# Stick-breaking attention moved beside the RWKV prelude, and the queued projections multiplied unsplit in fp32

## Chip, core and metric

The kernel runs on one core of a Trainium2 chip, as one program. Its time is device microseconds (us) of one execution; the median of three executions is given. A core has TensorE (PE, matmuls and transposes), VectorE (DVE), ScalarE (ACT), GpSimd (POOL) and SyncE (SP, which issues most transfers here). Each engine runs its own instructions strictly in the order in which the program lists them.

## What is computed

Two blocks follow one another. Only the first is touched. It works on 272 rows (16 meta tokens and 256 tokens) of width 1024:

```python
xn = rms_norm(h, norm_mix[layer])
proj = xn @ w_in[layer]
q_sb, k_sb, v_sb, rw, gate_sb, gate_rw = jnp.split(proj, in_splits, axis=-1)
y_sb = stick_breaking_attention(...)          # 8 heads of 64
rw = token_shift(rw, mu_rw[layer])
r, kr, vr, w_lo, a_lo, g_lo = jnp.split(rw, rw_splits, axis=-1)
...                                           # decay, a, g, kk: the RWKV inputs
y_rw = rwkv7_recurrence(r_h, decay, k_h, v_h, kk, a_h)
y_rw = group_norm_heads(y_rw, ln_x_w[layer], ln_x_b[layer])   # + bonus, times g
merged = (sigmoid(gate_sb) * (y_sb @ w_sb_out[layer])
          + sigmoid(gate_rw) * (y_rw @ w_rw_out[layer]))
h = h + merged @ w_out[layer]                 # then a feed-forward layer
```

Stick-breaking attention, for a query t and a key s < t, weighs v_s with sigmoid(z_ts) times the product of (1 - sigmoid(z_tj)) over the keys between. The second block (two layers of attention and of a product-key expert layer) has the same work before and after.

## The kernel before

A tile scheduler turns the program's text into one fixed list of instructions for each engine; it decides by program order and by a few raised priorities, when the program is built.

**Split projections.** `proj_ws_steps` (L264 to L266) multiplies a weight matrix with the activations. Each step loads 512 KB of weights into a tile `raw` (three buffers). ACT copies it to `hi` in the shorter format fp32r (L221), and DVE (or POOL, with `sub=G`) subtracts to get `lo` (L222). The activations are held as the pair XH, XL in the same way. Every product is three matmuls: XH with hi, XL with hi, XH with lo. With 256 columns such a matmul reads `128x256`, for the 272 rows `128x272`.

**Stage 1, projections and attention.** q, k and v are projected first. Then the four pairs of heads of the stick-breaking attention run: scores (L518 to L525, 256-column products into the PSUM tile `w`), softplus as Abs, Exp, Ln on ACT (L527 to L529) and one DVE instruction, weights (L539), exponent (L549), output (L555 to L560) and a split of it into YH, YL. Between them the queue `K.queue` puts steps of the projections of kr, rr and vr (`FILL = 0, 2, 1` steps at three places of each pair).

**Stage 2, the RWKV prelude.** The last projection, LO (columns 3072 to 3359), gives the low-rank inputs of decay, a and g. Sigmoids (L642), a scan, exponents (L660 to L663), the inverse norm by Ln and Exp (L178, L179) and many elementwise products on DVE give the operands of the recurrence; transposes (L710, L715) and ACT copies end it. Beside it runs the queue with `gate(3360, gs)`, `merge_sb()` and `gate(4384, gr)`: 480 split matmuls in all, called the filler below. Its hi copies are on ACT, its lo subtractions on POOL. The filler's results leave PSUM through a sigmoid on ACT (L593) or a DVE product (L598).

**Stage 3, pairs.** Sixteen groups of products of ART with BZ or KZ (L743), masked by DVE, with the small matmuls of a block inverse between. **Stage 4, inverse chain.** The reduced blocks go to DRAM and back (`d_in`, `MI`), 15 pairs of DVE instructions (L767, L768) invert them row by row, and the result goes to DRAM and back (`d_out`, `XC`); then DVE masks it into TT (L867). **Stage 5, chunk chain.** Unit products (L874), then per 32-row chunk L920, a DVE sum (L921), L930, a DVE sum (L933) and so on, at the end a group norm (L977 to L988) whose result feeds the projection `w_rw_out`. The queue's matmuls stand between the others in stages 2 to 5, wherever the scheduler put them.

Of the kernel before, what the change touches and what calls it, by code (L numbers as in the profile page):

```python
# [8 lines left out]
F = mybir.dt.float32  # L9
FR = mybir.dt.float32r  # L10
# [8 lines left out]
NM = 16  # L19
S = 256  # L20
# [108 lines left out]


FILL = 0, 2, 1
# [5 lines left out]
class Kit:  # L137
# [133 lines left out]

    def proj_nat(self, w, KT, xh, xl, pj, groups, keep=(), done=None, sub=None, gate=(), loaded=None, free=0, idle=0):
# [109 lines left out]
def block1(tc, A, K, dump, finish, outer):  # L382
# [4 lines left out]
    with ExitStack() as es:  # L387
        ps1 = es.enter_context(ExitStack())
        pj = ps1.enter_context(tc.tile_pool(name="pj", bufs=4, space=PSUM))
# [74 lines left out]


        with tc.tile_pool(name="sb", bufs=1) as sb, tc.tile_pool(name="pw", bufs=2, space=PSUM) as pw:
            def wtile():
                return pw.tile([128, 2, 512], F, name="w", tag="w")

            CB = const_part(sb, "end1", "end2", "csb")  # L470
            identb = sb.tile([128, 128], BF, name="identb")
            V.tensor_copy(identb, ident)
            negb = sb.tile([128, 128], BF, name="negb")
            V.tensor_copy(negb, CB("neg"))
            qT = sb.tile([128, 4, S], F, name="qT")
            KZ = sb.tile([128, 2, 4, T], F, name="KZ")
            G.memset(KZ[64:128, 0], 0.0)
            G.memset(KZ[0:64, 1], 0.0)
            KM = sb.tile([128, 4, 128], F, name="KM")
            VM = sb.tile([128, 4, 128], F, name="VM")  # L480
# [12 lines left out]
            K.proj_ws(win, [(1024, 512)], 8, 2, xhT, xlT, T, SUB, lambda j, ps: SC.activation(vTs[:, j], ps, AF.Copy), pj)
            for par in range(2):
                ps = slice(64 * par, 64 * par + 64)
                V.tensor_copy(KM[ps, :, 16 * par:16 * par + 16], KZ[ps, par, :, 0:NM])
                V.tensor_copy(VM[ps, :, 16 * par:16 * par + 16], vTs[ps, :, 0:NM])
            w = wtile()
            for i in range(2):
                for p in range(4):  # L500
                    PE.transpose(w[:, i, p * 128:(p + 1) * 128], vTs[:, p, NM + 128 * i:NM + 128 * (i + 1)], ident)
            V.tensor_copy(VS[:, 0], w[:, 0])
            SC.activation(VS[:, 1], w[:, 1], AF.Copy)
            w = wtile()
            for p in range(4):
                PE.transpose(w[:, 0, p * 128:(p + 1) * 128], VM[:, p], ident)
            V.tensor_copy(VB, w[:, 0].rearrange("p (a b) -> p a b", b=128))
            for c0, dst, mu in ((2048, kr, 20), (1536, rr, 16), (2560, vr, 24)):
                K.queue.append(K.proj_ws_steps(win, [(c0, 512)], 8, 2, xhT, xlT, T, SUB, shift_into(lambda j, dst=dst: dst[:, j], mu), pj))
            ntri, nones = CB("ntri"), CB("nones")  # L510
            parts = lambda x: ([x[:, 256 * r:256 * r + 256] for r in range(2)], [x[:, 512 + 128 * r:640 + 128 * r] for r in range(2)], x[:, 768:1024])

            def sb_scores(p):
                wf = wtile().rearrange("p a b -> p (a b)")
                z0, z1, zm = parts(wf)
                q = qT[:, p]
                for r in range(2):
                    PE.matmul(z0[r], lhsT=KZ[:, r, p, NM:NM + 128], rhs=q, start=r == 0, stop=False)  # L518
                for r in range(2):
                    PE.matmul(z0[r][:, 0:128], lhsT=identb, rhs=negb, start=False, stop=r == 1)  # L520
                for r in range(2):
                    PE.matmul(z1[r], lhsT=KZ[:, r, p, NM + 128:NM + 256], rhs=q[:, 128:256], start=r == 0, stop=False)
                PE.matmul(zm, lhsT=KM[:, p], rhs=q, start=False, stop=False)
                for r in range(2):
                    PE.matmul(z1[r], lhsT=identb, rhs=negb, start=False, stop=r == 1)  # L525
                e = sb.tile([128, 1024], F, name="e", tag="e", bufs=2)
                SC.activation(e, wf, AF.Abs)  # L527
                SC.activation(e, e, AF.Exp, scale=-1.0)
                SC.activation(e, e, AF.Ln, bias=1.0)  # L529
                sp = sb.tile([128, 1024], F, name="sp", tag="sp", bufs=2)  # L530
                V.scalar_tensor_tensor(sp, wf, 0.0, e, op0=OP.max, op1=OP.add)
                return wf, sp

            def sb_weights(wf, sp):
                z0, z1, zm = parts(wf)
                s0, s1, sm = parts(sp)

                def acc(o, l, r, last=False):
                    PE.matmul(o, lhsT=l, rhs=r, start=False, stop=last, skip_group_check=True)  # L539

                for r in range(2):
                    acc(z0[r], ntri, s0[r])
                    acc(z0[r][:, 128:256], nones, s1[r], r == 1)
                    acc(z1[r], ntri, s1[r])
                    acc(zm, CB(f"non{r}"), s0[r])
                    acc(zm[:, 128:256], CB(f"non{r}"), s1[r])
                acc(zm, CB("ntri16"), sm, True)
                a = sb.tile([128, 1024], F, name="a", tag="a")
                SC.activation(a, wf, AF.Exp)  # L549
                return a  # L550

            def sb_out(p, wf, a):
                a0, a1, am = parts(a)
                y = wf[:, 0:S]
                PE.matmul(y, lhsT=VB[:, p], rhs=am, start=True, stop=False)  # L555
                for r in range(2):
                    hs = slice((2 * p + r) * 64, (2 * p + r) * 64 + 64)
                    yr = y[64 * r:64 * r + 64]
                    PE.matmul(yr, lhsT=VS[:, 0, hs], rhs=a0[r], start=False, stop=False)
                    PE.matmul(yr[:, 128:256], lhsT=VS[:, 1, hs], rhs=a1[r], start=False, stop=True)  # L560
                K.split(y, YH[:, p], YL[:, p])
# [12 lines left out]
        dump("ysbh", YH.bitcast(F))  # L574

        gT = b1.tile([128, 4, S], F, name="gT")
        gs = bl.tile([128, 8, S], F, name="gs", tag="gs")
        VN = b1.tile([128, 2, 512], F, name="VN", tag="VN")
        VW = b1.tile([128, 2, 512], F, name="VW")
        LB = b1.tile([128, 2, 2, 512], F, name="LB", tag="LB")  # L580
        RN = b1.tile([128, 2, 2, 8, 64], F, name="RN", tag="RN")
        QT = K.gp.tile([128, 2, 8, 128], F, name="QT", tag="h")
        RT = b1.tile([128, 2, 8, 128], F, name="RT", tag="RT")
        OT = b1.tile([128, 2, 8, 128], F, name="OT", tag="OT")
        pcb = b1.tile([128, 4, 8], F, name="pcb")
        S0 = b1.tile([128, 4, 64], F, name="S0")
        d_in = dr.tile([2, 8, 2048], F, name="d_in")
        d_out = dr.tile([2, 8, 2048], F, name="d_out")

        def gate(c0, dst):  # L590
            for g in range(2):
                K.queue.append(K.proj_ws_steps(win, [(c0 + 512 * g, 512)], 8, 2, xhX, xlX, S, SUB,
                          lambda j, ps, g=g: SC.activation(dst[:, 4 * g + j], ps, AF.Sigmoid), pj, sub=G))  # L593

        def merge_sb():
            for g in range(2):
# [1067 lines left out]
```

## Time and profile before

| what | before |
|---|---|
| time, median of three runs (lowest to highest) | 2433.31 us (2431.47 to 2433.57) |
| the profiled execution's own time | 2431.37 us |
| its span | 2429.6 us |
| mean granted TensorE clock, as a share of 2.4 GHz | 0.988 |
| busy in the span: PE, DVE, ACT, POOL | 2334.9, 1662.0, 1204.5, 241.5 us |

The table is of the whole program. The change touches the first 320 us or so of the span, and there the engines share the time differently than in the rest, so the rows below are read stage by stage. An fp32 matmul stands in the trace as two records, an fp32r matmul as one. The time from the start of one matmul to the start of the next, called its pitch below, is what a matmul costs an engine that is never waiting, because matmuls overlap.

### The profile page before, as it was taken

Reading aid. Unit: us, or ns where it says so; the run is one execution under the profiler, and the core shown is the slowest. Engines: PE = TensorE matmul, PEld = TensorE weight load, DVE = VectorE, ACT = ScalarE, POOL = GpSimd, SP = SyncE. Lnnn points to the kernel's source line nnn. Section 1 sums busy time; section 2 is a strip of 40 time slices with the busy share of each in tenths; the row PEclk is TensorE's granted clock in tenths of the full one; section 3 lists DMA queues with packets and bytes.
Section 4 is the critical chain, followed back from the end, with each engine's and each line's share of the span. In section 5 each row is a group of like instructions: output and inputs, shape, how many; then the busy total and the mean of one; then the engine's idle time right before and its main releaser. Section 6 shows DMA issues by size and latency. Waiting matters only on the chain.

```text
span 2429.6 us, 43499 instructions
## 1 busy us (share of the span) xinstructions
PE 2334.9 (96%) x17012; PEld 2111.7 (87%) x17012; DVE 1662.0 (68%) x3234; ACT 1204.5 (50%) x2118; POOL 241.5 (10%) x253
## 2 busy tenths in 40 slices
PE   8988989998999999999999999899999999999998
PEld 7877869987689999999888877689999999888886
DVE  4478555557779868886555556769968887555555
ACT  4663545444535555545545554534545544455453
POOL 0065400007300000000000003610000000000000
PEclk9998999999999999999999999999999999999999
DMA  5232136564235554545656565315555555555664
GB/s 178 87 110 77 57 122 191 183 202 151 79 113 180 184 175 159 166 156 190 195 194 192 195 201 183 121 62 166 187 181 163 165 159 182 190 191 192 197 192 147
DMA packets 145637, 389.68 MB, mean 160 GB/s; under 512 B 18731, under 2 KB 49510, under 8 KB 145174
## 3 DMA queue, kind: packets, MB, share of 16 engines
q1 hardware_dynamic: 140070, 375.34, 48.3%
q10 hardware_dynamic: 5360, 11.56, 1.5%
q8 instruction: 133, 2.18, 0.4%
q14 instruction: 74, 0.61, 0.1%
HBM read 385.34 MB, written 1.31 MB: 159 GB/s over the span
## 4 chain that ended last, share of the span: by engine, by line
PE 74%; DVE 7%; issue 4%; ACT 2%; DMA 2%; POOL 1%; DVEq 0%; ACTq 0%; POOLq 0%
PE w L1581 27%; PE a L1383 10%; PE a L1384 10%; PE a L1386 9%; PE pj L302 3%; PE w L1552 2%; PE pj L264 2%; PE pj L266 2%; DVE lo L222 2%; PE pj L265 2%; PE a L1304 2%; PE w L1421 1%; ACT hi L221 1%; DMA raw<-in_peer_v_dram 1%; PE o L1268 1%
## 5 line engine op out<-in xcount | busy, mean ns | idle before, releaser
L222 DVE TENSOR_TENSOR lo<-raw,hi 128x1024 fp32r<-128x1024 f32 (+1 forms) x656 | 792.6, 1210 | 543.0 <-ACT hi L221 540.0
L221 ACT ACTIVATE hi<-raw 128x1024 fp32r<-128x1024 f32 (+1 forms) x696 | 709.2, 1023 | 825.7 <-PE w L1581 314.3
L1383 PE MATMUL a<-XH,hi 128*128 128x256 f32 x2048 | 498.4, 283 | 2.5 <-ACT S L1389 1.5
L1384 PE MATMUL a<-XL,hi 128*128 128x256 f32 x2048 | 492.4, 280 | 0.0
L1581 PE MATMUL w<-hi,ww 128*128 128x512 f32 x1968 | 488.9, 390 | 3.3 <-ACT ww L226 3.2
L1581 PEld LDWEIGHTS w<-hi,ww 128*128 128x128 f32 x1968 | 369.0, 188 | 81.9 <-ACT ww L226 5.8
L1383 PEld LDWEIGHTS a<-XH,hi 128*128 128x128 f32 x2048 | 385.3, 188 | 6.4 <-DVE S L1392 3.6
L1384 PEld LDWEIGHTS a<-XL,hi 128*128 128x128 f32 x2048 | 385.9, 188 | 0.0
L1386 PE MATMUL a<-XH,lo 128*128 128x256 f32 x2048 | 287.1, 281 | 0.0
L1581 PE MATMUL w<-lo,ww 128*128 128x512 f32 x984 | 264.5, 390 | 0.0
L1386 PEld LDWEIGHTS a<-XH,lo 128*128 128x128 f32 x2048 | 259.3, 188 | 0.0
L1581 PEld LDWEIGHTS w<-lo,ww 128*128 128x128 f32 x984 | 184.3, 188 | 40.2 <-DVE lo L222 2.3
L173 POOL TENSOR_TENSOR ag<-ag,mhalf 128x1 f32<-128x1 f32 x10 | 9.8, 984 | 1830.7 <-DVE ag L349 1620.8
L264 PE MATMUL pj<-XH,hi 128*128 128x256 f32 (+1 forms) x424 | 123.7, 297 | 4.6 <-ACT gs L593 2.8
L266 PE MATMUL pj<-XH,lo 128*128 128x256 f32 (+1 forms) x424 | 116.8, 298 | 5.1 <-DVE lo L222 3.9
L265 PE MATMUL pj<-XL,hi 128*128 128x256 f32 (+1 forms) x424 | 121.4, 292 | 0.0
L227 DVE TENSOR_TENSOR ww<-S,ww 128x256 fp32r<-128x256 f32 x246 | 102.6, 418 | 0.0
L226 ACT ACTIVATE ww<-S 128x256 fp32r<-128x256 f32 x246 | 98.0, 399 | 0.0
L265 PE MATMUL pj<-big,hi 128*128 128x256 f32 x352 | 97.9, 284 | 0.0
L264 PE MATMUL pj<-big,hi 128*128 128x256 f32 x352 | 97.5, 284 | 0.0
L266 PE MATMUL pj<-big,lo 128*128 128x256 f32 x352 | 92.8, 283 | 0.0
L1389 ACT ACTIVATE S<-a 128x256 f32<-128x256 f32 (+18 forms) x248 | 75.7, 305 | 30.2 <-PE a L1386 30.1
(508 smaller groups left out, 3478.8 us busy)
## 6 DMA issues: line engine op xcount, KB each, us to landing
raw<-in_peer_u_dram SPq DMA_DIRECT2D x256, 512.0 KB
raw<-in_peer_v_dram SPq DMA_DIRECT2D x256, 512.0 KB
raw<-in_w_in_dram SPq DMA_DIRECT2D x58, 512.0 KB
raw<-in_w_ffn_in_dram SPq DMA_DIRECT2D x88, 256.0 KB
raw<-in_peer_wq_dram SPq DMA_DIRECT2D x32, 512.0 KB
raw<-in_w_ffn_out_dram SPq DMA_DIRECT2D x22, 512.0 KB
raw<-in_w_o_dram SPq DMA_DIRECT2D x16, 512.0 KB
raw<-in_w_out_dram SPq DMA_DIRECT2D x8, 512.0 KB
```

What stands on the lines that cost most here:

```text
L221: nc.scalar.activation(a, r, AF.Copy)
L222: (sub or nc.vector).tensor_sub(b, r, a.bitcast(F))
L226: self.nc.scalar.activation(hi, xf, AF.Copy)
L227: self.nc.vector.tensor_sub(lo, xf, hi.bitcast(F))
L264: PE.matmul(ps[j], lhsT=wh, rhs=xh(kk), start=kk == 0 and j % per == 0, stop=False)
L265: PE.matmul(ps[j], lhsT=wh, rhs=xl(kk), start=False, stop=False)
L266: PE.matmul(ps[j], lhsT=wl, rhs=xh(kk), start=False, stop=kk == KT - 1 and (j % per == per - 1 or j == len(subs) - 1))
L1383: PE.matmul(a, lhsT=hi[:, k], rhs=XH[:, k], start=k == 0, stop=False)
L1384: PE.matmul(a, lhsT=hi[:, k], rhs=XL[:, k], start=False, stop=False)
L1386: PE.matmul(a, lhsT=lo[:, k], rhs=XH[:, k], start=False, stop=k == 7)
L1389: SC.activation(o[:, n:], a[:, n:], AF.Gelu)
L1581: K.marks["v"] = PE.matmul(acc[t][:, n], lhsT=x[:, ts(t)], rhs=v[:, n * 512:(n + 1) * 512], start=f, stop=e)
```

## The change

1. The attention leaves stage 1. The projections kr, rr, vr and LO follow q, k, v at once; of the attention only the scores of the first two head pairs stand between them. The rest (weights, outputs, and the scores of pairs 2 and 3) runs in stage 2, beside the prelude. Its PSUM tile `w` is released before the filler's tiles exist, so the filler starts when the attention is over.
2. The filler no longer splits its weights. `proj_raw_steps` multiplies the fp32 weights as they are loaded with fp32 activations: 160 matmuls `128x256` in fp32 instead of 480 in fp32r. The hi copies on ACT and the lo subtractions on POOL for it fall away. The activations `XF` are XH + XL, two DVE sums; the attention's result Y stays fp32 and is written by one ACT copy.
3. To find room, e and a share the buffers of `hi`, SP those of RT, the values and small keys those of OT, KZa later becomes `gr`, and a scratch area for transfers is made smaller.

```diff
-FILL = 0, 2, 1
...
+    def proj_raw_steps(self, w, cols, KT, kper, x, N, subs, evac, pj):
...
+        for kb in range(0, KT, kper):
+            raw = self.raw()
...
+            for k in range(kper):
+                kk = kb + k
+                for j, s in enumerate(subs):
+                    PE.matmul(ps[j], lhsT=rv[:, k, s:s + 128], rhs=x(kk), start=kk == 0 and j % 2 == 0,
+                              stop=kk == KT - 1 and (j % 2 == 1 or j == len(subs) - 1))
...
             for c0, dst, mu in ((2048, kr, 20), (1536, rr, 16), (2560, vr, 24)):
-                K.queue.append(K.proj_ws_steps(win, [(c0, 512)], 8, 2, xhT, xlT, T, SUB, shift_into(lambda j, dst=dst: dst[:, j], mu), pj))
...
-            ahead = sb_scores(0)
-            for p in range(4):
-                wf, sp = ahead
-                if p < 3:
-                    ahead = sb_scores(p + 1)
-                K.fill(FILL[0])
-                a = sb_weights(wf, sp)
-                K.fill(FILL[1])
-                sb_out(p, wf, a)
-                K.fill(FILL[2])
-            K.fill()
...
+                K.proj_ws(win, [(c0, 512)], 8, 2, xhT, xlT, T, SUB, shift_into(lambda j, dst=dst: dst[:, j], mu), pq)
...
+            XF = [K.st.tile([128, 4, S], F, name="XF", tag="lo", bufs=K.nb[2]) for _ in range(2)]
+            for i, x in enumerate(XF):
+                V.tensor_add(x, XH[:, 4 * i:4 * i + 4, NM:T].bitcast(F), XL[:, 4 * i:4 * i + 4, NM:T].bitcast(F))
...
+            SP = b1.tile([128, 2, 1024], F, name="SP", tag="RT")
+            pws = rws.enter_context(ExitStack())
+            pw = pws.enter_context(tc.tile_pool(name="pw", bufs=2, space=PSUM))
...
+            ahead = sb_scores(0)
+            for p in range(4):
+                wf, sp = ahead
+                if p < 3:
+                    ahead = sb_scores(p + 1)
+                sb_out(p, wf, sb_weights(wf, sp))
+            dump("ysbh", Y)
+            pws.close()
+            pj = rws.enter_context(tc.tile_pool(name="pf", bufs=2, space=PSUM))
...
+        def gate(c0, dst):
+            for g in range(2):
+                K.queue.append(K.proj_raw_steps(win, [(c0 + 512 * g, 512)], 8, 2, lambda k: XF[k // 4][:, k % 4], S, SUB,
+                          lambda j, ps, g=g: SC.activation(dst[:, 4 * g + j], ps, AF.Sigmoid), pj))
...
-        gr = bl.tile([128, 8, S], F, name="gr", tag="YHL")
+        gr = sb.tile([128, 8, S], F, name="gr", tag="KZa")
...
-    nc = _bacc.Bacc("TRN2", target_bir_lowering=False, num_devices=1)
+    nc = _bacc.Bacc("TRN2", target_bir_lowering=False, num_devices=1, dynamic_dma_scratch_size=1024)
```

On ScalarE, in the prelude, before: from the sigmoids of a and decay (L642) to the inverse norm (L178, L179), with the filler's hi copies (L221) and sigmoids (L593) between.

```order
L660 ACT_TABLE_LOAD
L660 ACTIVATE t_P<-t_cs 128x1088
L662 ACTIVATE t_cs<-t_cs 128x1088
L663 ACTIVATE t_sg<-t_sg 128x1088
L221 ACTIVATE hi<-raw 128x512 x2
L178 ACT_TABLE_LOAD
L178 ACTIVATE ri<-t_X 128x1088
L593 ACT_TABLE_LOAD
L593 ACTIVATE gs<-pj 128x256 x2
L221 ACTIVATE hi<-raw 128x512
L179 ACT_TABLE_LOAD
L179 ACTIVATE ri<-ri 128x1088
```

The same place after the change; L596 to L599 are the exponents, L175 and L176 the inverse norm, L683 to L685 the attention's Abs, Exp and Ln, L706 its exponent and L718 the copy of its result.

```order
L596 ACT_TABLE_LOAD
L596 ACTIVATE t_P<-t_cs 128x1088
L718 ACTIVATE Y<-w 128x256
...
L683 ACTIVATE e<-w 128x1024
L706 ACTIVATE a<-w 128x1024
L175 ACT_TABLE_LOAD
L175 ACTIVATE ri<-t_X 128x1088
L684 ACT_TABLE_LOAD
L684 ACTIVATE e<-e 128x1024
L176 ACTIVATE ri<-ri 128x1088
L718 ACTIVATE Y<-w 128x256
L685 ACT_TABLE_LOAD
```

The attention's activations have moved in between the prelude's, and the filler's are gone from here; from the second copy of LO (L478) to the last of the prelude's copies the list now holds 13 table loads, where it held six.

On TensorE, in the chunk chain, before: the unit products (L874) and the chunk products (L920, L930, L942) of the second and third 32-row chunk.

```order
L874 MATMUL pj<-RN,TT 128x128 x8
L920 MATMUL pj<-Sbd_1800,WT 128x128 x2
L942 MATMUL pm<-RM,Sbd_1800 128x128
L920 MATMUL pj<-Sbd_1800,WT 128x128 x2
L942 MATMUL pm<-RM,Sbd_1800 128x128
L930 MATMUL pj<-UV_1804,LB 128x128 x4
L874 MATMUL pj<-Z_1928,OT 128x128 x8
L920 MATMUL pj<-Sbd_1801,WT 128x128 x2
```

The same place after the change, where L883 are the unit products, L929, L939 and L951 the chunk products, and L285 the unsplit filler.

```order
L883 MATMUL pj<-RN,TT 128x128 x8
L285 MATMUL pj<-XF,raw 128x256 x3
L929 MATMUL pj<-Sbd_1791,WT 128x128 x4
L951 MATMUL pm<-RM,Sbd_1791 128x128 x2
L285 MATMUL pj<-XF,raw 128x256 x8
L939 MATMUL pj<-UV_1795,LB 128x128 x4
L883 MATMUL pj<-Z_1919,OT 128x128 x8
L285 MATMUL pj<-XF,raw 128x256 x3
```

Before, no filler stands behind the first chunk; now it stands between the products of the first six. Of the 160 unsplit matmuls 28 stand among the pairs of stage 3, 36 in stage 4 and 96 behind the first unit product of stage 5; before, 55 of the 480 split ones stood in stage 3 and 56 in stage 5.

## Rows read from the trace of the kernel before

**Rows 1.** Windows by stage; the last two a gapless stretch and the feed-forward layer.

```profile
core 0: us, PE busy (x) PEld busy (x) DVE busy (x) ACT busy (x) POOL busy (x), PEclk, DMA share, GB/s
56.20:133.00 76.80, 75.21 (x559) 69.73 (x558) 35.29 (x65) 49.24 (x62) 3.68 (x6) 1.00 0.38 109
133.00:194.30 61.30, 48.96 (x318) 44.78 (x316) 47.90 (x48) 44.52 (x72) 48.37 (x35) 0.89 0.30 87
194.30:222.80 28.50, 28.40 (x169) 25.43 (x169) 21.31 (x61) 5.38 (x19) 6.14 (x5) 0.93 0.30 82
222.80:253.30 30.50, 23.20 (x153) 19.78 (x151) 21.18 (x44) 8.72 (x21) 19.72 (x18) 0.89 0.28 68
253.30:319.80 66.50, 53.77 (x425) 47.91 (x425) 34.77 (x86) 37.22 (x66) 21.37 (x40) 0.96 0.12 40
268.40:291.75 23.35, 23.01 (x196) 20.84 (x194) 13.63 (x34) 12.80 (x25) 8.14 (x18) 1.00 0.13 45
380.00:480.00 100.00, 100.00 (x836) 100.00 (x835) 54.33 (x67) 46.63 (x69) 0.00 (x0) 1.00 0.61 185
```

**Rows 2.** Timeline of PE, late in stage 5: start, us, names, count, idle before.

```profile
293.25 0.70 PE L980 MATMUL pm<-sqy,cst 128*128 128x256 f32 x2 [1.51 <-ACT sqy L978]
...
319.79 0.80 PE L264 MATMUL pj<-YRH,hi 128*128 128x256 f32 x2 [5.88 <-ACT YRH L226]
```

**Rows 3.** Timeline of PE, stage 2.

```profile
146.05 3.62 PE L648 MATMUL pj<-ls,wg 128*128 128x256 f32 x16
149.51 1.08 PE L671 MATMUL pj<-t_X,cst 128*128 128x272 f32 x4
...
157.21 0.39 PE L264 MATMUL pj<-XH,hi 128*128 128x256 f32 x1 [1.83 <-ACT gs L593]
...
158.26 0.42 PE L266 MATMUL pj<-XH,lo 128*128 128x256 f32 x1
158.47 0.42 PE L264 MATMUL pj<-XH,hi 128*128 128x256 f32 x1
```

**Rows 4.** Lines, PE in stage 1: count, busy us, mean ns, idle before.

```profile
L264 PE MATMUL pj<-XH,hi 128*128 128x272 f32 x121 | 35.6, 299 | 0.9 <-ACT pb L459 0.9
```

**Rows 5.** Timeline of PE, stage 1.

```profile
64.67 1.03 PE L518 MATMUL w<-qT,KZ 128*128 128x256 f32 x4
...
66.69 1.08 PE L518 MATMUL w<-qT,KZ 128*128 128x256 f32 x4
```

**Rows 6.** Timeline of ACT, stage 2, one table load.

```profile
139.15 1.28 ACT L636 ACT_TABLE_LOAD   x1
140.45 0.66 ACT L636 ACTIVATE ls<-ls 128x544 f32<-128x544 f32 x1
```

**Rows 7.** Lines, ACT in stage 2.

```profile
L221 ACT ACTIVATE hi<-raw 128x512 fp32r<-128x512 f32 x22 | 12.7, 624 | 8.6 <-POOL lo L222 4.3 <-issue 2.5 <-PE pj L265 1.8
...
L723 ACT ACTIVATE LB<-pj 64x512 f32<-64x512 f32 x4 | 2.4, 592 | 0.1
...
L660 ACT ACTIVATE t_P<-t_cs 128x1088 f32<-128x1088 f32 x1 | 1.1, 1110 | 0.0
```

**Rows 8.** Lines, DVE in stage 2.

```profile
L182 DVE SCALAR_TENSOR_TENSOR ri<-ri 128x1088 f32<-128x1088 f32 x1 | 2.3, 2316 | 0.0
...
L181 DVE SCALAR_TENSOR_TENSOR ri<-ri,t_X 128x1088 f32<-128x1088 f32 x1 | 1.3, 1292 | 0.0
```

**Rows 9.** Timeline of DVE, stage 4.

```profile
227.04 0.95 DVE L767 TENSOR_TENSOR tm<-XI,MI 128x1 f32<-128x1 f32 x1 [2.68 <-DMA MI<-d_in]
...
237.36 1.63 DVE L767 TENSOR_TENSOR tm<-XI,MI 128x81 f32<-128x81 f32 x1
...
243.01 0.40 DVE L767 TENSOR_TENSOR tm<-XI,MI 128x144 f32<-128x144 f32 x1
...
246.37 0.39 DVE L768 TENSOR_REDUCE XI<-tm 128x15 f32<-128x225 f32 x1
...
252.47 0.69 DVE L867 TENSOR_TENSOR TT<-XC,cst 128x512 f32<-128x512 f32 x1 [3.38 <-DMA XC<-d_out]
```

More of the change, by code (lines that the diff above doesn't have):

```diff
@@ L463, in shift_into, with bank @@
             return ev
[L466 to L480, printed above, removed]
+        def bank():
+            return pq.tile([128, 512], F, name="pj", tag="pj")
@@ new lines, in block1, with big @@
+        sb = bs.enter_context(tc.tile_pool(name="sb", bufs=1))
+        CB = const_part(sb, "end1", "end2", "csb")
+        identb = sb.tile([128, 128], BF, name="identb")
+        V.tensor_copy(identb, ident)
+        negb = sb.tile([128, 128], BF, name="negb")
+        V.tensor_copy(negb, CB("neg"))
+        qT = sb.tile([128, 4, S], F, name="qT")
+        KZa = sb.tile([128, 2, 4, T], F, name="KZa", tag="KZa")
+        G.memset(KZa[64:128, 0], 0.0)
+        G.memset(KZa[0:64, 1], 0.0)
+        with tc.tile_pool(name="rwp", bufs=1) as rw:
+            def big(tag):
+                return rw.tile([128, 4, T], F, name=tag, tag=tag)
+            VKM = b1.tile([128, 2048], F, name="VKM", tag="OT")
+            VS = VKM[:, 0:1024].rearrange("p (a b) -> p a b", b=512)
+            VB, KM = (VKM[:, c:c + 512].rearrange("p (a b) -> p a b", b=128) for c in (1024, 1536))
+            VM = rw.tile([128, 4, 128], F, name="VM", tag="t_X")
@@ L502, in block1 @@
-            V.tensor_copy(VS[:, 0], w[:, 0])
-            SC.activation(VS[:, 1], w[:, 1], AF.Copy)
-            w = wtile()
+                    PE.transpose(w[:, p * 128:(p + 1) * 128], vTs[:, p, NM + 128 * i:NM + 128 * (i + 1)], ident)
+                if i:
+                    SC.activation(VS[:, i], w, AF.Copy)
+                else:
+                    V.tensor_copy(VS[:, i], w)
+            w = bank()
             for p in range(4):
-                PE.transpose(w[:, 0, p * 128:(p + 1) * 128], VM[:, p], ident)
@@ L507, in block1 @@
[L507 removed]
+                PE.transpose(w[:, p * 128:(p + 1) * 128], VM[:, p], ident)
+            V.tensor_copy(VB, w.rearrange("p (a b) -> p a b", b=128))
             for c0, dst, mu in ((2048, kr, 20), (1536, rr, 16), (2560, vr, 24)):
[L509 to L511 removed]
@@ L513, in sb_scores @@
[L513 to L561, printed above, removed]
@@ L587, in block1 @@
[L587 to L596, printed above, removed]
-                K.queue.append(K.proj_ws_steps(A["w_sb_out"][0], [(512 * g, 512)], 4, 2, lambda k: YH[:, k], lambda k: YL[:, k], S, SUB,
-                          lambda j, ps, g=g: V.tensor_mul(gs[:, 4 * g + j], gs[:, 4 * g + j], ps), pj, sub=G))
@@ L614, in block1 @@
+            d_in = dr.tile([2, 8, 2048], F, name="d_in")
+            d_out = dr.tile([2, 8, 2048], F, name="d_out")
             CP = const_part(rw, "end0", "end1", "cp")
@@ new lines, in sb_weights, with acc @@
+            def sb_weights(wf, sp):
+                z0, z1, zm = parts(wf)
+                s0, s1, sm = parts(sp)
+                def acc(o, l, r, last=False):
+                    PE.matmul(o, lhsT=l, rhs=r, start=False, stop=last, skip_group_check=True)
+                for r in range(2):
+                    acc(z0[r], ntri, s0[r])
+                    acc(z0[r][:, 128:256], nones, s1[r], r == 1)
+                    acc(z1[r], ntri, s1[r])
+                    acc(zm, CB(f"non{r}"), s0[r])
+                    acc(zm[:, 128:256], CB(f"non{r}"), s1[r])
+                acc(zm, CB("ntri16"), sm, True)
+                a = K.st.tile([128, 1024], F, name="a", tag="hi", bufs=K.nb[1])
+                SC.activation(a, wf, AF.Exp)
+                return a
@@ new lines, in sb_out @@
+            def sb_out(p, wf, a):
+                a0, a1, am = parts(a)
+                y = wf[:, 0:S]
+                PE.matmul(y, lhsT=VB[:, p], rhs=am, start=True, stop=False)
+                for r in range(2):
+                    hs = slice((2 * p + r) * 64, (2 * p + r) * 64 + 64)
+                    yr = y[64 * r:64 * r + 64]
+                    PE.matmul(yr, lhsT=VS[:, 0, hs], rhs=a0[r], start=False, stop=False)
+                    PE.matmul(yr[:, 128:256], lhsT=VS[:, 1, hs], rhs=a1[r], start=False, stop=True)
+                SC.activation(Y[:, p], y, AF.Copy)
@@ L727, in values, with mbank @@
+            OT = b1.tile([128, 2, 8, 128], F, name="OT", tag="OT")
+            def mbank():
+                return pm.tile([128, 512], F, name="pm", tag="pm")
             def values(t, p, Nt):
```

95 lines of the change are left out of this document (59 added, 36 removed).

## The prediction

> **What bounds the kernel now.** I read the page first and then went stage by stage, since an average over the span says little about 300 us of it. The windows [rows 1] come first; the reader is to see which engine fills each stage. Stage 1 (from the end of q, k, v to the last LO matmul) takes 76.8 us, and PE is busy for 75.2 of them. Stage 2, the prelude up to the first pair, takes 61.3 us; PE, DVE, ACT and POOL are all busy for 44 to 49 us there, so a chain through them sets its length, and PE has 12 us to spare. Stage 3 is PE alone (28.4 of 28.5). Stage 4 waits for DVE's inverse chain and two trips through DRAM. In stage 5 the stretch from 268.4 to 291.75 holds no filler and no gap (23.0 of 23.35); the few waits come later, 1.5 us at one group-norm product and 5.9 us before the last projection [rows 2]. So PE sets stages 1, 3 and most of 5, and in those every PE instruction more is time more.
>
> **What a matmul costs.** In the feed-forward layer 836 fp32r matmuls of 256 columns fill 100 us: 0.1196 us each [rows 1], and 272 columns, in proportion, 0.127. Eight fp32 matmuls of 256 columns (16 records) take from 146.05 to 149.51: 0.4325 us each [rows 3]. The filler therefore grows from 480 x 0.1196 = 57.4 us of PE to 160 x 0.4325 = 69.2 us, 11.8 more. It used to lie in stages 2 (where PE had room) to 5; the question is where it lies now.
>
> **Step 1, stage 1 loses the attention.** There remain 3 x 121 split matmuls [rows 4] x 0.127 = 46.1 us, two score groups of 66.69 - 64.67 = 2.0 us [rows 5], twelve transposes of 1.3 us together (half of a 256-column pass each), 0.5 us of waits: 51.9 for 76.8, **-24.9**. ACT and DVE, at 49 and 35 us before with most of the attention among it, don't bind. The weights are some 15 loads of 512 KB in 52 us, about 150 GB/s, and 185 were reached elsewhere [rows 1].
>
> **Step 2, the attention beside the prelude.** The prelude keeps its own work, loses the filler, and gains four weight groups, two scores and four outputs on PE (about 23 us, with some 12 us of its own: PE is far from full), two DVE instructions for the softplus that remain, and above all ACT work. ACT works strictly in order, and the order interleaves the two. From the second copy of LO to the prelude's last copy its list holds 13 table loads of 1.28 us [rows 6], 16.7 us; 23 activations of 1024 to 1088 elements at about 1.06 (1.11 at 1088) [rows 7], 24.4; twelve copies of 512 elements at 0.59 [rows 7], 7.1; some twenty small ones at 0.4, 8: **56 us** without any wait. What it loses is 22 hi copies of 0.624 [rows 7]. DVE is relieved: the same kind of 1088-element instruction took 2.32 us beside POOL's subtractions and 1.29 without them [rows 8], and six or seven such stand in the prelude. But ACT, with 56 us that cannot be shortened and waits of 4 to 6 us along its list (for the weights of a pair, for the norm's matmuls), comes out at 60 to 62: I take **0** for the 61.3, with -5 (ACT without a wait) to +6 as ends.
>
> **Step 3, stage 3.** 28 unsplit for 55 split matmuls on a full PE: 12.1 - 6.6 = **+5.5**.
>
> **Step 4, the inverse chain.** It runs from 227.04 to 246.76. Its pieces are slow while POOL is busy (1.63 us for 81 elements) and fast after (0.40 for 144) [rows 9]. Without the filler's subtractions POOL keeps of its 19.7 us there [rows 1] the three products for the gates, so more than half of the slow-down should go, not all. All slow pieces at the fast ones' price would give 10.6 us for 19.7; none, 19.7. I take 14.2, **-5.5**, ends -9.1 and 0. Behind it nothing changes on the way through DRAM, except that SP now lists three filler loads ahead of `d_out`, the third waiting until PE has done 48 filler matmuls; PE gets there at about the time when the chain ends. One load of 512 KB takes 2.8 us at 185 GB/s: **+1**, ends 0 and 2.8. PE's 24 fillers behind the wait for Ubd must end before the first unit product, and they begin after a wait like that of before; some of them will run at half clock (below): **+1.7**, ends 0 and 3.4.
>
> **Step 5, the chunk chain.** 96 x 0.4325 = 41.5 us of filler for 56 x 0.1196 = 6.7: +34.8. The filler now stands between the products of six chunks, but in their stretch there was next to nothing to cover: the gaps are short of 0.4 us in 23 [rows 1], and the 1.5 us group-norm wait [rows 2] with some smaller ones behind it make 3. The 5.9 us at the end stay open, since no filler stands there. The sigmoids of the second gate now share ACT with the group norm's square roots, and the DVE products with the unit's copies, which I put at 2 us. **+33.8**, ends 28.8 and 36.8.
>
> **Sum:** -24.9 + 0 + 5.5 - 5.5 + 1 + 1.7 + 33.8 = **+11.6**. The profiled execution took 2431.4 us, so 2443.0; the median of the three runs stands 1.9 above it, so **2445 us**. In words: the filler moves from a stage where PE had 12 us to spare into one where it has none, and the time that stage 1 gives back is paid there.
>
> **The rule on table loads.** A table load starts at 139.15 and its activation 1.30 us later [rows 6], so a load costs 1.28 here. The Trainium skill (ScalarE: Activation LUTs, "What ACT_TABLE_LOAD costs") says that a switch costs a drain of about 1.38 us besides, 2.66 in all. By it the seven loads more would add 9.7 us to ACT, and the time would be near 2455, an estimate from that page. The trace does not agree with it.
>
> **Rivals.**
> *The clock* (slower still). After a wait of 1.83 us PE's matmuls go at a pitch of 0.21 instead of 0.12, that is at 1.2 GHz [rows 3], and the granted clock of stage 2 is 0.89 [rows 1]. With PE idle for a third of the prelude, the weights, outputs and transposes there may run at half clock throughout: twice 3.5 us of weights and 1.35 of output in each of two rounds of the attention, 10 us, of which ACT's own work hides half, +5, and +1.7 on the first pairs: 2452. For it: longer idle than before. Against: the attention's PE work isn't last.
> The Trainium skill (TensorE: Matmul & The Clock Gate, "What's actually happening") names the lower clock as the idle state that activity lifts; the row agrees.
> *Same.* ACT hardly waits (56, -5.3), the inverse chain loses all its slow pieces (-3.6 more) and `d_out` isn't held up (-1): 11.6 - 9.9 = +1.7, 2435.
> *Faster.* VectorE, not ScalarE, sets the prelude, and POOL's subtractions were what held it up. Seven wide instructions at 1.0 us less and some 5 us of PE's waits for the filler's results (1.83 at one of them [rows 3]) give a prelude near 49, -12; the inverse chain at 10.6 us gives -3.6 more, and neither clock nor `d_out` is lost (-2.7): 11.6 - 18.3 = -6.7, 2427. It decides if the prelude is under 49 us. Against: ACT's 56 us, which stand before the first pair all but the last copies. For: some of ACT's early rows may run before LO ends.
> *The drain* of the table loads, 2455.
>
> **How the numbers follow.** The sum's own case (2438 to 2451) has 0.46, the clock 0.15, the drain 0.03, same 0.20, faster 0.16. A measurement of this kernel tells 0.2%, 4.9 us, from no change, so faster ends at 2428.4 and slower begins at 2438.2: 0.16 faster, 0.20 same, 0.64 slower. All lower ends together give -4.7 (2428.6 to the median), all upper ones +29.6 (2463); these don't all come together, so 2429 to 2457.
>
> **What would show it.** Right: LO's last matmul near 108 us in the new trace; the first pair some 61 us behind it with 13 table loads and ACT busy for most of it; inverse pieces all under 1 us except beside three POOL products; from the first unit product to the projection `w_rw_out` about 100 us, with a full PE for the first 85. Wrong: a prelude under 50 us, or over 68; an unsplit matmul at another pitch than 0.43; a chunk chain under 92 us, which would mean that the filler covers waits that the records of before don't show.

## The result and the profile after

The changed kernel takes 2447.33 us (median of four runs, 2446.13 to 2450.02) where the kernel before took 2432.41 in the same session: 1.0059 of its time, 95% interval 1.0047 to 1.0071. It is slower by about 15 us; 12 were forecast, and the time lies inside the range. The windows of the changed kernel by stage follow (columns as in [rows 1]; the third is a piece of the second, the last a piece of the one above it).

```profile
56.90:108.70 51.80, 50.25 (x401) 49.53 (x399) 31.31 (x57) 24.64 (x37) 0.24 (x1) 1.00 0.54 152
108.70:170.00 61.30, 44.59 (x228) 35.74 (x229) 34.14 (x49) 52.87 (x65) 15.90 (x12) 0.83 0.02 4
145.40:165.40 20.00, 15.19 (x75) 12.04 (x76) 17.81 (x23) 15.57 (x19) 10.58 (x5) 0.74 0.00 1
170.00:202.70 32.70, 32.68 (x177) 29.20 (x178) 20.95 (x62) 4.94 (x18) 0.00 (x0) 1.00 0.20 51
202.70:227.40 24.70, 19.75 (x91) 15.17 (x90) 17.27 (x41) 4.71 (x13) 9.39 (x10) 1.00 0.34 88
227.40:329.40 102.00, 89.50 (x560) 80.46 (x560) 38.32 (x94) 39.69 (x73) 15.29 (x36) 0.94 0.27 82
227.40:291.50 64.10, 64.10 (x409) 59.09 (x410) 19.20 (x46) 16.54 (x39) 10.34 (x24) 0.97 0.31 90
```

Set beside [rows 1], and with the starts of the first pair, the last pair, the inverse chain, the first unit product and the projection `w_rw_out` in the two traces, the stages compare so:

| stage | before, us | after, us | change | forecast |
|---|---|---|---|---|
| end of stage 1 (last LO matmul) | 133.2 | 108.7 | -24.5 | -24.9 |
| prelude | 61.3 | 61.3 | 0 | 0 |
| pairs, first start to last end | 27.9 | 32.1 | +4.2 | +5.5 |
| reduced blocks through DRAM | 4.7 | 4.8 | +0.1 | 0 |
| inverse chain | 19.7 | 15.4 | -4.3 | -5.5 |
| from its end to the first unit product | 6.5 | 5.1 | -1.4 | +2.7 |
| chunk chain, to `w_rw_out` | 66.5 | 102.0 | +35.5 | +33.8 |
| start of `w_rw_out` | 319.8 | 329.4 | +9.6 | +11.6 |
| the rest of the span | 2109.8 | 2118.8 | +9.0 | 0 |

The table compares the two profiled executions, and its changes add up to 18.6 us, where the medians differ by 14.9: the profiled one of the changed kernel was the slowest of its four (2450.02 us). Experiment 6 comes back to the last row.

The reader is to see in the windows that the prelude has PE busy for 44.6 of 61.3 us with hardly a byte loaded (4 GB/s), and that PE is idle nowhere in the first 64 us of the chunk chain. The timeline of PE in that chain shows what fills it (start, us, line, names, count, idle before); 11 unsplit matmuls are 22 records.

```profile
249.14 1.05 PE L929 MATMUL pj<-Sbd,WT 128*128 128x128 f32 x8
250.03 4.91 PE L285 MATMUL pj<-XF,raw 128*128 128x256 f32 x22
254.78 1.05 PE L939 MATMUL pj<-UV,LB 128*128 128x128 f32 x8
...
304.99 0.71 PE L939 MATMUL pj<-UV,LB 128*128 128x128 f32 x4 [3.24 <-DVE UV L930]
...
329.42 0.80 PE L261 MATMUL pj<-YRH,hi 128*128 128x256 f32 x2 [5.87 <-ACT YRH L223]
```

From 250.03 to 254.78 eleven of them take 0.432 us each, as [rows 3] gave for the same shape. The wait of 5.87 before `w_rw_out` is the 5.88 of [rows 2]. The filler covers neither that nor the 3.24 us.

### The profile page after: what moved, and what is told of

The parts are those of the page before. It is cut to its first block, busy times and chain, and to the rows that moved or that the text cites. A ratio compares the mean times of both kernels' runs of the same rounds, so it can differ in the third digit from the quotient of the medians.

```text
span 2448.2 us, 43072 instructions
## 1 busy us (share of the span) xinstructions
PE 2345.7 (96%) x16852; PEld 2117.4 (86%) x16852; DVE 1642.7 (67%) x3232; ACT 1184.5 (48%) x2079; POOL 186.5 (8%) x213
## 4 chain that ended last, share of the span: by engine, by line
PE 81%; DVE 8%; ACT 4%; DMA 3%; issue 2%; POOL 1%; ACTq 0%; DVEq 0%; SPq 0%; POOLq 0%
PE w L1600 26%; PE a L1402 10%; PE a L1403 10%; PE a L1405 9%; PE pj L322 3%; PE pj L261 3%; PE pj L263 3%; PE pj L262 3%; PE w L1571 2%; DVE lo L219 2%; PE pj L285 2%; PE a L1323 2%; DMA raw<-in_peer_v_dram 1%; PE w L1440 1%; ACT hi L218 1%
## 5 line engine op out<-in xcount | busy, mean ns | idle before, releaser
L218 ACT ACTIVATE hi<-raw 128x1024 fp32r<-128x1024 f32 (+1 forms) x656 | 686.0, 1047 | 815.0 <-PE w L1600 314.1
L261 PE MATMUL pj<-XH,hi 128*128 128x272 f32 (+1 forms) x296 | 84.8, 295 | 0.9 <-ACT hi L218 0.9
L1556 DVE TENSOR_TENSOR E<-iotah,ID 128x1024 f16<-128x1024 f16 x128 | 82.1, 684 | 3.5 <-PE w L1571 3.2
L262 PE MATMUL pj<-XL,hi 128*128 128x272 f32 (+1 forms) x296 | 84.0, 291 | 0.0
```

The costliest lines, as they stand in the source:

```text
L218: nc.scalar.activation(a, r, AF.Copy)
L261: PE.matmul(ps[j], lhsT=wh, rhs=xh(kk), start=kk == 0 and j % per == 0, stop=False)
L262: PE.matmul(ps[j], lhsT=wh, rhs=xl(kk), start=False, stop=False)
L1556: V.tensor_tensor(row(k), io, val(ID[:, 1 - k]), op=OP.is_equal)
```

## The experiments

Two theories stood against each other. **Where the filler lies:** PE pays for a filler matmul in the stages that it fills, and nothing in those where it waits; the change took the filler out of the prelude and put it into the chunk chain. **fp32 work:** the loss is the 11.8 us by which 160 unsplit matmuls outlast 480 split ones, wherever they lie. Times are medians, ratios those against runs of the kernel before on the same chip.

**1. Unsplit alone.** The kernel before, with `proj_raw_steps`, XF and an fp32 Y, but with the attention left in stage 1.

```diff
-                K.split(y, YH[:, p], YL[:, p])
+                SC.activation(Y[:, p], y, AF.Copy)
...
-                K.queue.append(K.proj_ws_steps(win, [(c0 + 512 * g, 512)], 8, 2, xhX, xlX, S, SUB,
+                K.queue.append(K.proj_raw_steps(win, [(c0 + 512 * g, 512)], 8, 2, lambda k: XF[k // 4][:, k % 4], S, SUB,
```

> The kernel before with one part of the change alone: the filler multiplies unsplit in fp32, the attention stays in stage 1. Theory 'where the filler lies' (PE pays for a filler matmul only in the stages that it fills): all 160 now stand ahead of the first unit product, 95 of them in the prelude; stage 1 as before, prelude 55 to 61 us for 61.3, pairs +3, inverse chain about 4 us shorter, chunk chain about 6.7 us shorter: 2420 to 2430 us, faster than before. Rival 'fp32 work' (the 11.8 us of extra PE work are the loss, the attention's move is neutral): 2442 to 2446 us.

Measured: 2425.56 us, ratio 0.9973 (0.9962 to 0.9983). It is faster than before. Its windows:

```profile
56.00:133.00 77.00, 76.12 (x567) 70.79 (x566) 35.70 (x64) 49.08 (x62) 2.23 (x4) 1.00 0.40 110
133.00:189.70 56.70, 53.49 (x261) 46.12 (x260) 35.23 (x50) 33.90 (x50) 14.36 (x12) 1.00 0.34 97
189.70:220.50 30.80, 30.80 (x168) 27.16 (x168) 21.75 (x64) 2.41 (x14) 0.00 (x0) 1.00 0.26 70
220.50:245.20 24.70, 22.42 (x102) 17.48 (x100) 17.62 (x41) 4.12 (x12) 8.96 (x10) 1.00 0.41 108
245.20:307.60 62.40, 47.02 (x368) 40.31 (x368) 33.80 (x85) 35.52 (x64) 16.57 (x37) 0.98 0.10 33
```

The prelude holds 95 unsplit matmuls (41 us). From the end of LO's last matmul (132.6 us here) it is 57.1 us long, 4.2 shorter than before, with the granted clock at 1.00 throughout; the chain without filler is 62.4 us long. The rival's 2442 or more is out: unsplit fp32 is no loss by itself. What gains here is the unsplit product together with the casts and subtractions that fall away; no run separates the two. The traced execution was the fastest of eight (2419.80 us), so its windows show more than the median's gain.

**2. The move alone.** The changed kernel with the gates split again.

```diff
-                K.queue.append(K.proj_raw_steps(win, [(c0 + 512 * g, 512)], 8, 2, lambda k: XF[k // 4][:, k % 4], S, SUB,
-                          lambda j, ps, g=g: SC.activation(dst[:, 4 * g + j], ps, AF.Sigmoid), pj))
+                K.queue.append(K.proj_ws_steps(win, [(c0 + 512 * g, 512)], 8, 2, xhX, xlX, S, SUB,
+                          lambda j, ps, g=g: SC.activation(dst[:, 4 * g + j], ps, AF.Sigmoid), pj, sub=G))
```

> The changed kernel with the two gates' 128 unsplit matmuls made into 384 split ones again (the attention's own 32 stay unsplit): the attention's move nearly alone. Theory 'where the filler lies': 37.7 us of filler stay in the chunk chain for 41.5, pairs 3.8 us shorter, inverse chain some 4 us longer because POOL subtracts again: 2441 to 2446 us, still slower than before. Rival 'fp32 work': 9.4 us of PE work less than in the changed kernel, 2436 to 2439 us, close to before.

Measured: 2444.91 us, ratio 1.0055 (1.0037 to 1.0073), within the first theory's range and above the rival's; the inverse chain takes 19.0 us. The move alone loses 12 of the 15 us.

**3. Softplus earlier.** The tile e leaves the buffers of `hi`.

```diff
-                e = K.st.tile([128, 1024], F, name="e", tag="hi", bufs=K.nb[1])
+                e = EE[:, p % 2]          # EE has the space of gs
```

> The changed kernel with the softplus tile e in the space of gs in place of the buffers of hi, so that ScalarE can work on pairs 0 and 1 during the projections. The weights of both then stand in stage 1, the attention ends sooner, and the order has 41 filler matmuls ahead of the first pair (none before) and 45 in the chunk chain (96 before). Theory 'where the filler lies': chunk chain 22 us shorter, stage 1 about 7 us longer (two weight groups), prelude 55 to 61 us: 2425 to 2433 us. Rival 'table loads' (ScalarE's 13 loads set the loss): the order still has 12 in about the same place, so nothing is gained in the prelude, and 2440 us or more.

Measured: 2431.95 us, ratio 0.9997 (0.9988 to 1.0007), level with before. The attention ends at 152.9 us in place of 168.1, the filler starts beside the prelude, and the chain is 78.1 us long. Stage 1 ends at 114.8, the prelude takes 62 us again, one more than expected. The rival's 2440 or more is out.

**4. Filler in the prelude.** One PSUM buffer for the attention, so that the filler's exist beside it.

```diff
-            pw = pws.enter_context(tc.tile_pool(name="pw", bufs=2, space=PSUM))
+            pj = rws.enter_context(tc.tile_pool(name="pf", bufs=2, space=PSUM))
+            pws = rws.enter_context(ExitStack())
+            pw = pws.enter_context(tc.tile_pool(name="pw", bufs=1, space=PSUM))
```

> The changed kernel with one PSUM buffer for the attention in place of two, so that the filler's two PSUM tiles exist from the prelude on: the order has 68 filler matmuls ahead of the first pair and 18 in the chunk chain (0 and 96 before). The head pairs of the attention then run one after another. Theory 'where the filler lies': chunk chain 34 us shorter, stage 1 two us shorter, prelude 61 to 72 us since the attention is a serial chain now: 2412 to 2425 us, faster than before. Rival 'fp32 work' (PE's extra work is lost wherever it lies): at best 2440 us. Rival 'the attention's chain' (its latency in the prelude is what costs): prelude over 80 us, 2435 us or more.

Measured: 2440.73 us, ratio 1.0039 (1.0024 to 1.0054). The chain shrank to 69.5 us as forecast, but the gain was given back ahead of it, so the expected 2412 to 2425 us did not come. The rival on the attention's chain had this, though its 80 us are met only by the attention's end and not by the first pair:

```profile
179.67 3.77 PE L697 MATMUL w<-SP,csb 128*128 128x256 f32 x22 [2.80 <-DVE SP L689]
...
194.72 5.43 PE L697 MATMUL w<-SP,csb 128*128 128x256 f32 x22 [4.11 <-DVE SP L689]
...
203.09 0.40 PE L718 MATMUL w<-a,VKM 128*64 128x128 f32 x4
```

These are PE's weights of pairs 2 and 3, and its last output: the attention, pair after pair, ends at 203.5 us, 98 us after LO, and the last product of stage 3 only at 226.9, 57 us after the first pair, for 32 in the changed kernel. The 'at best 2440 us' of 'fp32 work' fits this time as well; it is experiment 1 that rules that theory out.

With these four, and the kernels below, the chain's length can be read against the filler in it:

| kernel | filler in the chunk chain | its PE time, us | chain, us |
|---|---|---|---|
| unsplit alone | none | 0 | 62.4 |
| before | 56 split | 6.7 | 66.5 |
| filler in the prelude | 18 unsplit | 7.8 | 69.5 |
| softplus earlier | 45 unsplit | 19.5 | 78.1 |
| move alone | 200 split, 32 unsplit | 37.7 | 97.0 |
| changed kernel | 96 unsplit | 41.5 | 102.0 |

Of the last kernel's 41.5 us of filler 39.6 are in the chain's length: 95%, and 81 to 92% in the other unsplit or mixed ones; the 56 split ones of before add 4.1 us for their 6.7. Part of this can be the clock: in the traces 13.3 us of the changed kernel's chain were at 1.2 GHz, and 2.2 of the chain without filler. If PE set all of that time, half of the difference, 5.5 us, is not the filler's, and its share is 82%. What it covers is little because of where it stands. Without filler PE is idle for 15.4 of 62.4 us; in the changed kernel it is idle for 12.5 of 102.0, and the last filler ends at 299.4 us, with only 0.2 of the idle time ahead of 300.9.

**5. The PSUM pools in the other order.** This is for the 9.0 us behind `w_rw_out`, which no step of the forecast had.

```diff
-            pj = rws.enter_context(tc.tile_pool(name="pf", bufs=2, space=PSUM))
             pm = rws.enter_context(tc.tile_pool(name="pm", bufs=2, space=PSUM))
+            pj = rws.enter_context(tc.tile_pool(name="pf", bufs=2, space=PSUM))
```

> The changed kernel with the two lines that open the PSUM pools pf and pm in the other order. Up to the projection w_rw_out every engine's order is that of the changed kernel; behind it PE's order is that of the kernel before again, where the changed kernel differs at w_out, in the feed-forward layer and in the second attention. Theory 'two losses' (some 10 us up to w_rw_out, and some 5 behind it, from the PSUM banks that the later stages inherit): w_rw_out starts near 329 us as in the changed kernel, the offset against before stays that up to the end, 2440 to 2443 us. Rival 'one loss' (what is lost behind w_rw_out is the clock's phase from run to run): no change, 2446 to 2449 us.

Measured: 2445.82 us, ratio 1.0060 (1.0046 to 1.0073): no difference to the changed kernel that the runs can tell, and not the 2440 to 2443 of 'two losses'. In the trace a small one stands. In the changed kernel PE waits 1.5 us at the first matmul of `w_out`, until a DVE product (L1041) has read a result out of PSUM; the kernels of experiments 2 to 4 have the same wait, this one and the kernel before don't:

```profile
344.79 0.71 PE L322 MATMUL pj<-hi,XH 128*128 128x512 f32 x2 [1.49 <-DVE gr L1041]
```

**6. The kernel before, once more.**

> The kernel before once more, for a second trace of it. Behind w_rw_out it took 2109.8 us in its first trace, while eight of the nine other kernels took 2113 to 2119 there, some with the same order of PE's instructions. Theory 'run to run' (how much of that stretch falls into stretches of half clock differs between executions): 2110 to 2117 us this time. Rival 'its own' (something in the kernel before makes it shorter there): 2109 to 2111 us again.

Measured: 2114.0 us behind `w_rw_out`, for 2109.8 in the first trace. The two traces hold the same instructions; the windows of the stretch around the second attention, of the first trace and of this one, differ in the clock:

```profile
1470.00:1590.00 120.00, 106.23 (x586) 84.99 (x585) 85.11 (x173) 56.24 (x145) 61.30 (x63) 0.97 0.40 131
```
```profile
1470.00:1590.00 120.00, 108.28 (x581) 86.68 (x580) 80.81 (x165) 55.55 (x139) 61.39 (x62) 0.94 0.41 134
```

Summed over the stretches that the trace gives at the lower clock, 31.1 us behind `w_rw_out` were at 1.2 GHz in the first execution and 38.7 in the second; with half of that taken off, as if PE set all of this time, 2094.3 and 2094.6 us remain. The changed kernel had 40.1 us at the lower clock, and 2098.8 remain. So of the 9.0 us some 4.5 are by this estimate the clock, which moves from execution to execution. Of the other 4.5 only the 1.5 us wait is seen to go with the pool order. The same sum gives 2093.2 for the other pool order, 2094.5 for the unsplit filler alone and 2094.1 to 2097.4 for the four kernels of experiment 7, which all have PE's order of before in this stretch; and it gives 2096.5, 2094.6 and 2096.0 for experiments 2 to 4, which open pf ahead of pm as the changed kernel does. The two groups overlap, and the medians (2445.82 and 2447.33) don't separate them either, so the remaining 3 us stay open.

**7. The gates' products held back.** Two attempts at GpSimd's part in the inverse chain. In the first the products were only listed later:

> As e6_pool_order, and GpSimd's three products for the gates are issued behind the last piece of the inverse chain, where they ran beside its pieces. Theory 'GpSimd slows VectorE' (a VectorE piece beside a GpSimd product takes 1.8 to 2.2 us for 0.2 to 0.3): inverse chain 10.6 us for 15.4, and 3 to 5 us off the end, 2436 to 2439 us. Rival 'the slow pieces are slow by themselves' (small ones at the chain's start, or PE's fillers): inverse chain still about 15 us, no change against e6_pool_order.

> As e1_unsplit_alone, with the gates' products behind the inverse chain. Theory 'GpSimd slows VectorE': inverse chain 10.6 us for 15.0, but PE holds 42 filler matmuls and 8 us of its own work in that stage and is busy for 22.4 of 24.7 us, so no more than 2 to 3 us come off: 2421 to 2424 us. Rival (the chain's length passes to the end whole): 2420 us or less.

Measured: 2445.93 us (1.0057, 1.0043 to 1.0071) and 2425.84 (0.9977, 0.9968 to 0.9986). The inverse chains took 15.4 and 15.0 us: GpSimd had nothing to wait for and ran the products at the same place. They tell nothing of GpSimd, but repeat experiments 5 and 1, with medians within 0.3 us of theirs. The second attempt gives the products a factor that is written late:

```diff
+        gcol = m.tile([128, 8], F, name="gcol")
+        V.tensor_copy(gcol, vT[:, 51:59])
...
-            b = lambda c: vT[:, c:c + 4].unsqueeze(2).to_broadcast([128, 4, S])
+            b = lambda c: gcol[:, c - 51:c - 47].unsqueeze(2).to_broadcast([128, 4, S])
```

> e7_gates_late did not do what its text says: the order allowed it, but nothing made GpSimd wait, and the three gate products ran beside the inverse chain as before. Here they read a small copy of their factors that is written only when the chain's tiles are free again, so they stand behind the chain's end. Otherwise as e6_pool_order. Theory 'GpSimd slows VectorE': inverse chain 10.6 us for 15.35 and the first unit product as much earlier, if PE's filler is done by then (36 matmuls, 15.6 us, and 8 us of its own work from the last pair on): 2441 to 2443 us for 2445.8. Rival 'slow by themselves': chain still about 15 us, 2445 to 2447 us.

> As e1_unsplit_alone with the same hold on the gate products (e8_unsplit_alone_gates_late did not hold them). Theory 'GpSimd slows VectorE': chain 10.6 us for 15.0; PE is busy for 22.4 of the 24.7 us of that stage, so 2 to 3 us come off the end: 2422 to 2424 us for 2425.7. Rival 'slow by themselves': no change.

Measured: 2440.71 us (1.0034, 1.0022 to 1.0047) and 2424.75 (0.9964, 0.9950 to 0.9978). The first is just under the expected 2441 to 2443, the second above the expected 2422 to 2424. In the changed kernel DVE's pieces and GpSimd's products stood so:

```profile
209.03 1.77 DVE L776 TENSOR_TENSOR tm<-XI,MI 128x16 f32<-128x16 f32 x1
...
211.04 2.21 DVE L776 TENSOR_TENSOR tm<-XI,MI 128x25 f32<-128x25 f32 x1
...
213.49 1.75 DVE L776 TENSOR_TENSOR tm<-XI,MI 128x36 f32<-128x36 f32 x1
...
215.50 0.24 DVE L776 TENSOR_TENSOR tm<-XI,MI 128x49 f32<-128x49 f32 x1
```
```profile
208.86 1.90 POOL L975 TENSOR_TENSOR KRV<-KRV,vT 128x1024 f32<-128x1024 f32 x1 [41.92 <-DVE tm L776]
210.84 2.35 POOL L976 TENSOR_TENSOR KRV<-KRV,gT 128x1024 f32<-128x1024 f32 x1
213.27 1.90 POOL L977 TENSOR_TENSOR gT<-gT,vT 128x1024 f32<-128x1024 f32 x1
```

and with the products held, the same pieces:

```profile
207.11 0.18 DVE L776 TENSOR_TENSOR tm<-XI,MI 128x16 f32<-128x16 f32 x1
...
207.53 0.20 DVE L776 TENSOR_TENSOR tm<-XI,MI 128x25 f32<-128x25 f32 x1
...
207.99 0.22 DVE L776 TENSOR_TENSOR tm<-XI,MI 128x36 f32<-128x36 f32 x1
```

Each slow piece lies beside one GpSimd product and lasts until it ends; without it a piece takes about a tenth. The chain is 10.6 us for 15.4, and 5.1 us come off the end. With the unsplit filler alone the chain is 10.7 us, but PE's filler then ends at 242.7 us, with the first unit product at 244.1, and only about 1 us comes off, which the runs don't tell from nothing.

**8. The first gate split on VectorE.** 64 unsplit matmuls of experiment 7's second kernel (2425.84 us) as 192 split ones, their subtractions on DVE.

```diff
-        gate(3360, gs)
+        gate_split(3360, gs)      # proj_ws_steps with xhX, xlX, no sub=G
```

> As e8_unsplit_alone_gates_late, with the first gate's 64 unsplit matmuls made into 192 split ones again, their lo subtractions on VectorE (1024 columns at a time) in place of GpSimd. PE work 64 x 0.4325 = 27.7 us becomes 192 x 0.1196 = 23.0. Theory 'PE is full in every stage now': 3 to 5 us shorter, 2417 to 2421 us. Rival 'VectorE's chain sets the prelude' (8 subtractions of 1.2 us more on it): prelude 60 us or more for 56.7, 2425 us or more.

Measured: 2427.65 us (0.9982, 0.9973 to 0.9991), nothing gained over 2425.84: the expected 3 to 5 us were wrong, and the time is the rival's. The prelude took 59.3 us for 57.1, just under the rival's 60, with DVE busy for 44.7 of them and PE for 56.0. From the first pair to the first unit product it took 58.2 for 56.0. Whether DVE's longer list or something else took back the 4.7 us of PE work is not shown; a part of this prelude was at 1.2 GHz too (granted clock 0.97 in it, 1.00 in the other).

**9. Fewer table loads.** The Ln of the softplus as a second Exp; the softplus is thereby left out.

```diff
-                SC.activation(e, e, AF.Ln, bias=1.0)
+                SC.activation(e, e, AF.Exp, scale=-1.0)
```

> As e6_pool_order, with the attention's Ln replaced by a second Exp of the same size: the softplus is left out of the computation, and seven of ScalarE's 13 table loads in the prelude fall away (9.0 us of ScalarE), every other engine's order staying the same. Theory 'ScalarE's list sets the prelude' (56 us of it without a wait): prelude 51 to 54 us for 60.9, 2436 to 2439 us. Rival 'VectorE's chain sets it' (its wide instructions in order, with ScalarE's activations between): prelude 58 to 61 us, 2443 us or more. Rival 'drain' (a switch costs 2.66 us, not 1.28): prelude 42 to 46 us, under 2432 us.

Measured: 2442.02 us (1.0036, 1.0022 to 1.0051) against 2445.82 of experiment 5. Seven table loads fewer, 9.0 us of ACT, and the prelude, counted from the start of LO's last matmul, went from 60.9 to 58.2 us. Its window:

```profile
107.60:166.20 58.60, 44.06 (x235) 34.73 (x233) 33.80 (x49) 44.05 (x58) 17.38 (x12) 0.88 0.00 1
```

ACT is busy for 44.1 us of it, as long as PE. Of 9.0 us 2.7 came off: ACT's list does not set the prelude by itself. The prelude is as long as the rival on VectorE's chain had it, and the time 1 us under its 2443. The drain, with 42 to 46 us, is out as well.

## Why the prediction was right, step by step

**The number is in part luck.** 2445 was forecast and 2447.3 measured. Up to `w_rw_out` the traces show +9.6 for +11.6; the medians differ by 14.9, so some 5 us lie in a stretch that the sum put at nothing. These two misses have opposite signs. What was foreseen is where the filler goes and that it is paid there.

**The sum's main part held.** The move from a stage with idle PE to one without any is shown by experiments 1 to 4: the attention's move alone costs 12, the unsplit filler alone gains 7, and the chain of the changed kernel grows by 0.82 to 0.95 of the filler put into it. Step 5 was sized 33.8 and measured 35.5. The 3 us that I let the filler cover did not come: PE was idle for 12.7 us of the chain before and for 12.5 after, 3.24 of them in a wait for DVE a few products behind the last filler. The full PE lasted for the first 73 us of the chain and not for the 85 that I had named.

**Step 1** (-24.9, measured -24.5) and **step 3** (+5.5, measured +4.2) were right. In step 3 the pairs of before ran partly at the lower clock (0.93 in [rows 1]) and those of after at 1.00, which the sum left out.

**Step 2 had the right length for a reason that was half right.** 0 was forecast and 0 measured. ACT was busy for 52.9 of the 61.3 us, near the 56 that I had added up. But experiment 9 shows that the list is not the bound by itself. The time passes from engine to engine: at the start PE waits 4.9 us for the first weights, whose softplus ACT ends at 112.3 us behind a table load and DVE at 113.6; then DVE waits 6.8 us for the inverse norm, and from 145.4 to 165.4 DVE is busy for 17.8 of 20 us. How much each of these sets is not shown. The rows, for ACT, DVE and PE (PE's row names a DVE memset that ends with the softplus):

```profile
109.97 1.28 ACT L685 ACT_TABLE_LOAD   x1
111.27 1.06 ACT L685 ACTIVATE e<-e 128x1024 f32<-128x1024 f32 x1
```
```profile
112.36 1.23 DVE L688 SCALAR_TENSOR_TENSOR SP<-w,e 128x1024 f32<-128x1024 f32 x1 [0.87 <-ACT e L685]
...
142.81 1.29 DVE L177 TENSOR_TENSOR ri<-ri 128x1088 f32<-128x1088 f32 x1 [6.80 <-ACT ri L176]
```
```profile
113.64 5.50 PE L696 MATMUL w<-SP,csb 128*128 128x256 f32 x20 [4.94 <-DVE pb L477]
```

The load takes 1.28 us again and its activation starts 1.30 us behind it, as [rows 6] had it. The Trainium skill (ScalarE: Activation LUTs, "What ACT_TABLE_LOAD costs") adds a drain of about 1.38 us; neither this trace nor experiment 9 shows it.

**Step 4 was mis-sized at its end.** The inverse chain came out at -4.3 for -5.5; three GpSimd products alone cost it 4.8 us (experiment 7), more than I left them. The +1 for `d_out` and +1.7 for PE's filler were wrong. In the changed kernel Ubd is ready at 206.2, ahead of the chain and not in its midst, so PE has its 48 matmuls done at 215.6 and all 64 at 222.4, before the chain's result is back; it then waits 5.0 us for the first unit product. DVE's and PE's rows:

```profile
205.50 0.69 DVE L844 TENSOR_TENSOR Ubd<-Um,cp 128x512 f32<-128x512 f32 x1
...
226.50 2.50 DVE L876 TENSOR_TENSOR TT<-XC,cst 128x512 f32<-128x512 f32 x4 [2.08 <-DMA XC<-d_out]
```
```profile
211.82 10.63 PE L285 MATMUL pj<-XF,raw 128*128 128x256 f32 x48
227.40 3.62 PE L883 MATMUL pj<-RN,TT 128*128 128x128 f32 x16 [4.95 <-POOL UV L864]
```

**What no step had:** the stretch behind `w_rw_out`. Of its 9.0 us in the traces some 4.5 are by estimate the clock's spread between executions and 1.5 the wait that goes with the order in which PSUM pools are opened; 3 stay open (experiments 5 and 6). Nor did the sum have the clock in the chunk chain: 13.3 us of it were at 1.2 GHz after the change, and 5.3 before.

**The rivals.** *The clock* came in part: the prelude's granted clock fell to 0.83 and 20 us of it were at 1.2 GHz, with the first weights at 5.3 us for 3.5, but the length stayed 61.3; what it would be at the full clock no run shows. *Faster* needed a prelude under 49 us; with POOL's subtractions gone and the attention left in stage 1 (experiment 1) it is still 57.1, PE being busy for most of it. *Same* needed an inverse chain of 10.6, which takes GpSimd's products away too.

**A version that beats both.** Unsplit filler with the attention left in stage 1: 2425.6 to 2425.8 us in two sets of runs, and 2424.75 with the gates' products held (the two are not told apart). The one half of the change is a gain of 7 to 8 us, the other a loss of 12. They don't add up: together they lose 15, not 5. Behind the move the unsplit filler is a loss of its own, since it stands among the pairs and in the chunk chain. Against the move alone it costs 4.0 us and 5.0 us there and saves 3.6 in the inverse chain, in the traces.

## What to carry to other kernels

Before a block of work is moved to fill one stage's idle engine, ask what filled that engine there until now, and where that goes: here the attention took the filler's place, and the filler went into a part of a chain whose matmuls already followed each other nearly without a gap. The price of a displaced filler is read from the window of the stage that receives it, not from the busy share of the program. A combined change is best tried by halves; the halves here had opposite signs, and their sum was not the whole.

## What was not expected of the hardware

A VectorE product of 16 to 36 elements took 1.75 to 2.21 us, for 0.18 to 0.22, when it lay beside a GpSimd product of 1024 columns; in these three cases it ended when the GpSimd instruction did. Two executions of one program differed by 4.2 us in a stretch of 2110 us; one had 7.6 us more of it at 1.2 GHz, which by half of that time accounts for 3.8.
